# Moving the tiles of a two-layer decoder trunk to other SBUF addresses: one common start offset modulo 512 bytes

## The chip, the core and the metric

One core of a Trainium2 chip runs the whole program in one launch. The metric is the device time of that launch in microseconds (us). The profile is one profiled execution; its own time and its span (first to last instruction) are given below, beside the median of three timed runs.

## What is computed

A decoder trunk of two layers on 256 tokens of width 1024, in float32. Every sub-layer sits between two RMS norms.

```python
for l in range(2):
    h = h + 0.5 * norm(swiglu(norm(h), w_gate, w_up, w_down))    # FFN 1, width 2816
    h = h + norm(concat[pool, rglru, nsa](norm(h) @ w_in) @ w_out)  # mixer
    h = h + 0.5 * norm(swiglu(norm(h), w_gate, w_up, w_down))    # FFN 2
swiglu = (silu(x @ w_gate) * (x @ w_up)) @ w_down
```

The mixer has three branches: a causal pooling, a gated recurrence behind a short convolution, and an attention with eight heads (compressed keys, and two branches over the raw keys). The two FFNs of each layer hold nearly all of the arithmetic.

## The kernel before, in words

**Matmuls in three passes.** Each float32 operand of a large product is split into a high part (the value rounded to the format that TensorE reads at full rate, float32r) and a low part (the rest). A product is then high·high, high·low and low·high, three matmuls into one PSUM bank. `mm3` (L245) issues them as L248, L249, L250; the forms with the weights as stationary operand write the same three in a loop (L378 in `gu_cols`, L791 in `chan`). Every matmul loads its own stationary operand (128 by 128) and streams a moving operand past it.

**Which tile is which operand.** `gu_rows` (L336, tiles `pg`, `pu`) and `proj` (L544, tiles `q`, `kv`, `kw`) hold the activations `xT` stationary and stream the weights `unit`: 256 columns for `pg` and `pu`, 512 for `q` and `kv`, 280 for `kw`. `gu_cols` (L369, tiles `qg`, `qu`) and `chan` (L776, tiles `chp`, `chr`, `chg`) hold the weights `unit` stationary and stream `xT`, 256 columns in two pieces of 128 (512 bytes each). `down` (L396, tile `facc`) and `out_mm` (L899, tile `oacc`) hold `hT`, `yA`, `yL` or `yP` stationary and stream 512 columns of `unit`. Transposes (`xt`, `ht`, `pT` and others) stream the identity `ident`, which is the first 128 columns of `cn`, past 128 columns of data. The scores of the attention start with a bf16 matmul (L729) that streams `maskb` past `identb`.

**Weights.** `fetch` (L198) brings 1 MB of a weight matrix into one of three `raw` buffers on SyncE's queue; `prepare` (L212) splits it into a `unit` of a ring of five: ScalarE writes the high part (L224), VectorE the low part (L225). `pump` refills as units are released. TensorE's order is written out by hand in strings (`MIXER_ORDER`, `FFN_FIRST`, `FFN_START`, `FFN_BODY`, `FFN_END`).

**Where tiles lie.** Each tile pool takes one stretch of every partition's SBUF, in the order in which the pools are opened (L91 to L94: `cst`, `rawp`, `ringp`, `wk`), and inside a pool the tiles follow one another in the order of their first use, each size rounded up to 32 bytes. The pools begin at byte 1152 (128 modulo 512), behind a scratch area and four constants. So a tile of odd size shifts all that lie behind it. By the allocator's list of the program before, the starts modulo 512 are:

| tiles | start modulo 512 |
|---|---|
| `x0`, `x1`, `cn` (2440 bytes, the first odd size) | 128 |
| `xT` (behind `identb`, `maskb`, `caddb`, `mhalf`) | 192 |
| `gpre`, `gpost`, `kT`, first `qT` and `vv`, `bd_*` | 32 |
| second `qT` and `vv` | 128 |
| `raw`, `unit`, `yP`, `yL`, the work tiles `w0` to `w5`, the `ht` buffers (`hT`, `yA`, `pr`, `Xm`) | 224 |
| `xg`, `fg` | 352 |
| `pT` | 160 |

Slices taken from these tiles for the large matmuls are multiples of 512 bytes apart, so each operand has its tile's start modulo 512.

Of the kernel before, what the change touches and what calls it, by code (L numbers as in the profile page):

```python
# [10 lines left out]
F32 = mybir.dt.float32  # L11
F32R = mybir.dt.float32r
BF16 = mybir.dt.bfloat16
I32 = mybir.dt.int32
# [5 lines left out]
P = 128  # L20
D = 1024
KD = D // P
S = 256
NT = S // P
# [62 lines left out]
def trunk(ctx: ExitStack, tc: tile.TileContext, T, out):  # L87
    nc = tc.nc
    pe, act, dve, pool = nc.tensor, nc.scalar, nc.vector, nc.gpsimd

    cst = ctx.enter_context(tc.tile_pool(name="cst", bufs=1))  # L91
    rawp = ctx.enter_context(tc.tile_pool(name="rawp", bufs=RAW))
    ringp = ctx.enter_context(tc.tile_pool(name="ringp", bufs=RING))
    wk = ctx.enter_context(tc.tile_pool(name="wk", bufs=1))  # L94
    psp = ctx.enter_context(tc.tile_pool(name="psp", bufs=8, space=PSUM))
    ctx.enter_context(tc.manual_schedule(engines={pe.engine}))

# [10 lines left out]
        return wk.tile([P, 1024], dtype, tag="ht", name=name, bufs=5)  # L108

    def small(name, n, bufs=2):  # L110
        return wk.tile([P, n], F32, tag=name, name=name, bufs=bufs)


    x = [cst.tile([P, D], F32, name=f"x{t}") for t in range(NT)]
    cn = cst.tile([P, C_COLS], F32, name="cn")
    ident = cn[:, C_ID:C_ID + P]
    identb = cst.tile([P, P], BF16, name="identb")
    maskb = cst.tile([P, P], BF16, name="maskb")
    caddb = cst.tile([P, NT, 32], BF16, name="caddb")
    mhalf = cst.tile([P, 1], F32, name="mhalf")  # L120
    pool.memset(mhalf, -0.5)
    xT = cst.tile([P, 2, NT, KD, P], F32R, name="xT")

    def gain(kind, ap, queue=nc.sync):
        g = cst.tile([P, D], F32, tag="g" + kind, name="g" + kind)
        queue.dma_start(g, ap.partition_broadcast(P))
        return g

# [315 lines left out]

    prm = cst.tile([P, 2, 18], F32, name="prm")
    pe2 = cst.tile([P, DEPTH, 16], F32, name="pe2")
    cs = cst.tile([P, NT, 2, 32], F32, name="cs")
    lc = cst.tile([P, DEPTH, 2], F32, name="lc")
    hb = cst.tile([P, 2, 4], F32, name="hb")
    bd = {n: cst.tile([P, 2, P], F32, name="bd_" + n) for n in ("pool_w", "lru_w_r", "lru_w_i")}  # L450
    O_CW, O_CB, O_BR, O_BI, O_LAM, O_PS = 0, 8, 10, 12, 14, 16

    def load_mixer(l):
# [5 lines left out]
    def load_setup():  # L459
        rows = wk.tile([P, 256], F32, tag="yP", name="rows")  # L460
        r = 0
        for ap in (T["conv_w"].rearrange("l j c -> (l j) c"), T["conv_b"], T["lru_b_r"], T["lru_b_i"],
                   T["lru_lambda"], T["pool_scale"]):
            nc.sync.dma_start(rows[r:r + ap.shape[0], :], ap)
            r += ap.shape[0]
        per = wk.tile([32, P], F32, tag="yL", name="per")
        nc.sync.dma_start(per, T["cmp_pe"].rearrange("l (a b) d -> (l a) (b d)", b=2))
        posi = wk.tile([2, P], I32, tag="v2", name="posi")
        nc.sync.dma_start(posi, T["positions"].rearrange("o (t p) -> (o t) p", t=NT))
        return rows, per, posi  # L470

# [56 lines left out]
    def mixer(l, rs, finish):  # L528
        if l:
            load_mixer(l)  # L530
        tab, qT, gates, vsw, accs, kwps, tmp = {}, {}, {}, {}, {}, {}, {}
        kT = [cst.tile([P, 2, (t + 1) * P], F32, tag=f"kT{t}", name="kT") for t in range(NT)]
        X2 = [wk.tile([P, 2, 272], F32, tag=f"v{i}", name="X2") for i in range(2)]
        for q in X2:
            pool.memset(q[:, :, 256:272], 0.0)

# [34 lines left out]
        def q_tr(t):  # L571
            q = tmp.pop(("q", t))
            b = bank("qT")
            for i in range(4):
                pe.transpose(b[:, i * P:(i + 1) * P], q[:, i * P:(i + 1) * P], ident)
            qT[t] = cst.tile([P, 4, P], F32, tag=f"qT{t}", name="qT")
            act.activation(qT[t], b.rearrange("p (i c) -> p i c", i=4), AF.Copy)

        def kv_rope(t):
            tb, kw = tab[t], kwps[t]  # L580
            kv = accs["kv", t]
            A = w(3 * t, "kA")[:, :384].rearrange("p (h f) -> p h f", f=32)
            B = w(3 * t + 1, "kB")[:, :384].rearrange("p (h f) -> p h f", f=32)
            src = kv.rearrange("p (a x h f) -> p a x h f", a=2, x=2, f=32)[:, :, 0]
            for q, c in ((A, 2), (B, 3)):
                dve.tensor_mul(q[:, :8].rearrange("p (a h) f -> p a h f", a=2), src,
                               tb[:, c:c + 1, None, :].to_broadcast([P, 2, 4, 32]))
                dve.tensor_mul(q[:, 8:12], kw[:, :P].rearrange("p (h f) -> p h f", f=32),
                               tb[:, c:c + 1, :].to_broadcast([P, 4, 32]))
            vc = wk.tile([P, 2, 2, 64], F32, tag="pT", name="vc", bufs=4)  # L590
            act.activation(vc, kv[:, 128:256].rearrange("p (v d) -> p v d", v=2)[:, :, None, :]
                           .to_broadcast([P, 2, 2, 64]), AF.Copy, scale=rs[t][0])
            vv = cst.tile([P, 2, P], F32, tag=f"vv{t}", name="vv")
            act.activation(vv[:, 0, :], kv[:, 384:512], AF.Copy, scale=rs[t][0])
            act.activation(vv[:, 1, :], kw[:, P:2 * P], AF.Copy, scale=rs[t][0])
            vsw[t] = vv
            A = A.rearrange("p (h b) f -> p h b f", b=2)
            B = B.rearrange("p (h b) f -> p h b f", b=2)
            K = w(3 * t + 2, "kr")
            ksw = K[:, :256].rearrange("p (h b f) -> p h b f", b=2, f=32)  # L600
            dve.tensor_sub(ksw[:, :, 0, :], A[:, 2:6, 0, :], B[:, 2:6, 1, :])
            dve.tensor_add(ksw[:, :, 1, :], A[:, 2:6, 1, :], B[:, 2:6, 0, :])
            kc = K[:, 256:512].rearrange("p (v u b f) -> p v u b f", v=2, u=2, f=32)
            bc = [P, 2, 2, 32]
            dve.tensor_sub(kc[:, :, :, 0, :], A[:, 0:2, None, 0, :].to_broadcast(bc),
                           B[:, 0:2, None, 1, :].to_broadcast(bc))
            dve.tensor_add(kc[:, :, :, 1, :], A[:, 0:2, None, 1, :].to_broadcast(bc),
                           B[:, 0:2, None, 0, :].to_broadcast(bc))
            hrs = small("hr", 1)
            pool.tensor_scalar(hrs, rs[t][0], 0.5, None, op0=ALU.mult)  # L610
            g = cst.tile([P, 8, 3], F32, tag=f"gt{t}", name="gt")
            act.activation(g, kw[:, 256:280].rearrange("p (h b) -> p h b", b=3), AF.Tanh, scale=hrs)
            pool.tensor_scalar(g, g, 0.5, 0.5, op0=ALU.mult, op1=ALU.add)
            gates[t] = g
            tmp["k", t] = K, vc
# [158 lines left out]
        Y, C = {}, {}  # L774

        def chan(nm, c):  # L776
            if c == 0:
                if nm == "g":
                    C[nm] = w(5, "gl").rearrange("p (c n) -> p c n", c=2)
                else:  # L780
                    C[nm] = wk.tile([P, 2, 272], F32, tag="v2" if nm == "p" else "v3", name="x" + nm)
                    pool.memset(C[nm][:, :, :16], 0.0)
            dst = C[nm][:, c, :] if nm == "g" else C[nm][:, c, 16:]
            b = bank("ch" + nm)[:, :S]
            u = units[l, nm, 0]
            b3 = b.rearrange("p (t n) -> p t n", t=NT)
            n = 0
            for k in range(KD):
                cs_ = slice(c * P, (c + 1) * P)
                for a, h in ((0, 0), (0, 1), (1, 0)):  # L790
                    pe.matmul(b3, u[:, a, k, cs_], xT[:, h, :, k, :], start=n == 0, stop=n == 3 * KD - 1)  # L791
                    n += 1
            if c == 1:
                done((l, nm, 0))
            dve.tensor_mul(dst, b, tmp["rsB"])

        def pool_in():
            xp = C["p"]
            A = wk.tile([P, 2, 272], F32, tag="v0", name="pA")
            B = wk.tile([P, 2, 272], F32, tag="v1", name="pB")  # L800
            pool.tensor_add(A[:, :, 1:], xp[:, :, 1:], xp[:, :, :271])
            pool.tensor_add(B[:, :, 3:], A[:, :, 3:], A[:, :, 1:270])
            pool.tensor_copy(A[64:, 0, 16:], B[64:, 0, 16:])
            pool.tensor_add(A[:, 1, 7:], B[:, 1, 7:], B[:, 1, 3:268])
            pool.tensor_add(B[64:, 1, 16:], A[64:, 1, 16:], A[64:, 1, 8:264])
            pool.tensor_copy(A[64:, 1, 16:], B[64:, 1, 16:])
            pool.tensor_mul(A[:, :, 16:32], A[:, :, 16:32],
                            cn[:, C_EDGE:C_EDGE + 32].rearrange("p (c n) -> p c n", c=2))
            C["d"] = A
# [206 lines left out]
```

## Time and profile before

| | |
|---|---|
| median of 3 timed runs | 989.61 us (985.83 to 989.83) |
| the profiled execution | 989.13 us |
| its span | 987.3 us |
| TensorE matmul busy | 967.7 us, 98% |
| VectorE, ScalarE, GpSimd busy | 66%, 49%, 8% |
| HBM traffic over the span | 177 GB/s |

Busy time of TensorE counts overlapping matmuls once, and a matmul's recorded duration (0.28 us for 256 columns) is longer than the distance to the next one's start, since matmuls are pipelined. What a stream of matmuls costs is therefore read from the distance of starts, which the timeline and the chain of waits give.

### The profile page before, as it was taken

To read this page: it belongs to the slowest core of one execution; us is meant where nothing else is said; L and a number is where in the kernel's file an instruction comes from. 1 tells how busy PE (TensorE), PEld (TensorE's weight loads), DVE (VectorE), ACT (ScalarE), POOL (GpSimd) and SP (SyncE) were. 2 spreads that over 40 slices of the span, in tenths; PEclk is the share of its full clock that TensorE was granted. 3 is DMA by queue.
4 is the path that set the end of the run, shared out by engine and by line. 5 is a ranking of instruction groups with operands and counts; after the bars stand their busy time and mean duration, and the time that the engine had idled before them with its cause. 6 is when DMAs were issued, how large, how long until landed. Compare 5 with 4: busy or idle time off the path is not lost.

```text
span 987.3 us, 16105 instructions
## 1 busy us (share of the span) xinstructions
PE 967.7 (98%) x6678; PEld 881.9 (89%) x6678; DVE 646.9 (66%) x864; ACT 479.3 (49%) x760; POOL 80.5 (8%) x136
## 2 busy tenths in 40 slices
PE   6999999999999999999999999999999999999997
PEld 5999999988779999999999999998887799999996
DVE  5785555678978655655676565667698777565552
ACT  5563443457556543434454443435477465343431
POOL 2000000030034000000030000003001320000000
PEclk9999999999999999999999999999998999999999
DMA  7975565457526655555456655554762157555511
GB/s 251 337 234 203 182 202 173 151 175 171 175 68 214 203 181 181 194 180 185 157 196 233 204 179 187 194 174 140 190 187 86 43 203 246 189 195 174 192 62 43
DMA packets 131553, 176.04 MB, mean 178 GB/s; under 512 B 13156, under 2 KB 111768, under 8 KB 131480
## 3 DMA queue, kind: packets, MB, share of 16 engines
q1 hardware_dynamic: 131192, 174.43, 54.9%
q8 instruction: 52, 0.85, 0.4%
q10 hardware_dynamic: 288, 0.59, 0.2%
q14 instruction: 21, 0.17, 0.0%
HBM read 173.95 MB, written 1.05 MB: 177 GB/s over the span
## 4 chain that ended last, share of the span: by engine, by line
PE 94%; DVE 2%; ACT 2%; DMA 1%; issue 0%; DVEq 0%; POOLq 0%; ACTq 0%; SPq 0%; POOL 0%
PE qu L378 21%; PE qg L378 21%; PE facc L250 8%; PE facc L249 8%; PE facc L248 8%; PE pu L248 2%; PE pu L250 2%; PE pu L249 2%; PE oacc L248 2%; PE oacc L249 1%; PE oacc L250 1%; PE pg L249 1%; PE pg L250 1%; PE pg L248 1%; PE yT L763 1%; PE chp L791 1%
## 5 line engine op out<-in xcount | busy, mean ns | idle before, releaser
L224 ACT ACTIVATE unit<-raw 128x1024 fp32r<-128x1024 f32 (+2 forms) x320 | 322.7, 1033 | 353.6 <-issue 296.6
L225 DVE TENSOR_TENSOR unit<-raw,unit 128x1024 fp32r<-128x1024 f32 (+2 forms) x320 | 375.9, 1195 | 139.8 <-ACT unit L224 139.5
L378 PEld LDWEIGHTS qg<-xT,unit 128*128 128x128 f32 x1728 | 208.9, 188 | 2.2
L378 PE MATMUL qu<-xT,unit 128*128 128x256 f32 x1728 | 210.7, 281 | 0.0
L378 PE MATMUL qg<-xT,unit 128*128 128x256 f32 x1728 | 210.3, 281 | 0.0
L378 PEld LDWEIGHTS qu<-xT,unit 128*128 128x128 f32 x1728 | 207.0, 188 | 0.0
L248 PE MATMUL facc<-unit,hT 128*128 128x512 f32 x352 | 137.7, 391 | 0.0
L250 PE MATMUL facc<-unit,hT 128*128 128x512 f32 x352 | 137.6, 391 | 0.0
L249 PE MATMUL facc<-unit,hT 128*128 128x512 f32 x352 | 137.5, 391 | 0.0
L250 PEld LDWEIGHTS facc<-unit,hT 128*128 128x128 f32 x352 | 66.1, 188 | 14.0
L248 PEld LDWEIGHTS facc<-unit,hT 128*128 128x128 f32 x352 | 66.2, 188 | 12.9
L249 PEld LDWEIGHTS facc<-unit,hT 128*128 128x128 f32 x352 | 66.1, 188 | 13.1
L388 DVE TENSOR_TENSOR gp<-qg,rsB 128x512 f32<-128x512 f32 x36 | 24.8, 690 | 65.0 <-PE qg L378 65.0
L264 POOL TENSOR_TENSOR mspost<-ev,s 128x1 f32<-128x1 f32 x8 | 4.7, 591 | 670.8 <-ACT sq L258 670.8
L393 DVE SCALAR_TENSOR_TENSOR h<-qu,m 128x512 f32<-128x512 f32 x36 | 24.9, 691 | 52.1 <-PE qu L378 52.1
L249 PE MATMUL pg<-unit,xT 128*128 128x256 f32 x128 | 36.9, 288 | 1.6 <-DVE unit L225 1.5
L248 PE MATMUL pg<-unit,xT 128*128 128x256 f32 x128 | 36.8, 287 | 0.4 <-ACT unit L224 0.4
L250 PE MATMUL pg<-unit,xT 128*128 128x256 f32 x128 | 36.3, 284 | 0.0
L248 PE MATMUL pu<-unit,xT 128*128 128x256 f32 x128 | 36.2, 282 | 0.0
L249 PE MATMUL pu<-unit,xT 128*128 128x256 f32 x128 | 35.8, 280 | 0.0
L250 PE MATMUL pu<-unit,xT 128*128 128x256 f32 x128 | 35.6, 278 | 0.0
L739 ACT ACTIVATE pr<-s,mx 128x128 f32<-128x128 f32 (+1 forms) x64 | 26.1, 433 | 3.7 <-DVE mx L737 3.6
(259 smaller groups left out, 1164.3 us busy)
## 6 DMA issues: line engine op xcount, KB each, us to landing
raw<-in_ffn_w_down_dram SPq DMA_DIRECT2D x44, 1024.0 KB, 5.4
raw<-in_ffn_w_gate_dram SPq DMA_DIRECT2D x42, 1024.0 KB, 5.2
raw<-in_ffn_w_up_dram SPq DMA_DIRECT2D x42, 1024.0 KB, 5.2
raw<-in_w_in_dram SPq DMA_DIRECT2D x14, 1024.0 KB, 5.1
raw<-in_w_out_dram SPq DMA_DIRECT2D x4, 1024.0 KB, 5.0
raw<-in_w_out_dram SPq DMA_DIRECT2D x8, 512.0 KB, 6.4
raw<-in_w_in_dram SPq DMA_DIRECT2D x4, 560.0 KB, 3.7
raw<-in_ffn_w_up_dram SPq DMA_DIRECT2D x4, 512.0 KB
```

The source lines that it names most:

```text
L224: act.activation(u[:, 0, i:i + step], r[:, i:i + step], AF.Copy)
L225: dve.tensor_sub(u[:, 1, i:i + step], r[:, i:i + step], u[:, 0, i:i + step].bitcast(F32))
L248: pe.matmul(o, sh, mh, start=first and i == 0, stop=False)
L249: pe.matmul(o, sh, ml, start=False, stop=False)
L250: pe.matmul(o, sl, mh, start=False, stop=last and i == n - 1)
L264: pool.tensor_add(m, eps, s2[:, 0:1])
L378: pe.matmul(o3, u[:, a, k, bs], xT[:, h, :, k, :], start=n == 0, stop=n == 3 * KD - 1)
L388: dve.tensor_tensor(b2(gp), b2(g), tmp["rsB"][:, None, :].to_broadcast([P, 2, S]), op=ALU.mult)
L393: dve.scalar_tensor_tensor(h, u, 0.5, m, op0=ALU.mult, op1=ALU.mult)
L739: act.activation(prs[v][:, b0 + i, :], sb[v][:, i, :], AF.Exp, bias=mx[:, i:i + 1], accum_out=cf[:, v, b0 + i:b0 + i + 1])
L763: pe.matmul(YT[t][v * 64:(v + 1) * 64, :], vsw[kb][:, br, v * 64:(v + 1) * 64], PT.pop((t, br, v, kb)), start=False, stop=br == 1 and kb == t,
L791: pe.matmul(b3, u[:, a, k, cs_], xT[:, h, :, k, :], start=n == 0, stop=n == 3 * KD - 1)
```

## The change

No instruction is added, removed or reordered; pools and the tiles' membership in them change. A new pool `lead` (416 bytes: `identb` 256, `caddb` 128, `mhalf` 4 rounded to 32) comes first, so that what follows begins at 1152 + 416 = 1568, which is 32 modulo 512. A new pool `big` comes behind it and holds tiles of `cst` whose sizes are multiples of 512; `rawp`, `ringp` and `wk` follow, `wk` without its odd-sized tiles; `cst`, with all odd sizes, is opened last. By these sizes every tile of `big`, `rawp`, `ringp` and `wk` starts at 32 modulo 512, and so does `cn`, the first tile of `cst`. `maskb`, `kk` and the tiles of the tags `v0` to `v3` lie behind `cn` at other offsets.

```diff
-    cst = ctx.enter_context(tc.tile_pool(name="cst", bufs=1))
+
+    lead = ctx.enter_context(tc.tile_pool(name="lead", bufs=1))
+    big = ctx.enter_context(tc.tile_pool(name="big", bufs=1))
     rawp = ctx.enter_context(tc.tile_pool(name="rawp", bufs=RAW))
     ringp = ctx.enter_context(tc.tile_pool(name="ringp", bufs=RING))
     wk = ctx.enter_context(tc.tile_pool(name="wk", bufs=1))
+    cst = ctx.enter_context(tc.tile_pool(name="cst", bufs=1))
...
     def small(name, n, bufs=2):
-        return wk.tile([P, n], F32, tag=name, name=name, bufs=bufs)
-
-
-    x = [cst.tile([P, D], F32, name=f"x{t}") for t in range(NT)]
+        return (wk if n % 128 == 0 else cst).tile([P, n], F32, tag=name, name=name, bufs=bufs)
+
+
+    identb = lead.tile([P, P], BF16, name="identb")
+    caddb = lead.tile([P, NT, 32], BF16, name="caddb")
+    mhalf = lead.tile([P, 1], F32, name="mhalf")
+    xT = big.tile([P, 2, NT, KD, P], F32R, name="xT")
+    x = [big.tile([P, D], F32, name=f"x{t}") for t in range(NT)]
     cn = cst.tile([P, C_COLS], F32, name="cn")
     ident = cn[:, C_ID:C_ID + P]
-    identb = cst.tile([P, P], BF16, name="identb")
     maskb = cst.tile([P, P], BF16, name="maskb")
-    caddb = cst.tile([P, NT, 32], BF16, name="caddb")
-    mhalf = cst.tile([P, 1], F32, name="mhalf")
     pool.memset(mhalf, -0.5)
-    xT = cst.tile([P, 2, NT, KD, P], F32R, name="xT")
...
-        g = cst.tile([P, D], F32, tag="g" + kind, name="g" + kind)
+        g = big.tile([P, D], F32, tag="g" + kind, name="g" + kind)
...
-    cs = cst.tile([P, NT, 2, 32], F32, name="cs")
+    cs = big.tile([P, NT, 2, 32], F32, name="cs")
...
-    bd = {n: cst.tile([P, 2, P], F32, name="bd_" + n) for n in ("pool_w", "lru_w_r", "lru_w_i")}
+    bd = {n: big.tile([P, 2, P], F32, name="bd_" + n) for n in ("pool_w", "lru_w_r", "lru_w_i")}
...
-        posi = wk.tile([2, P], I32, tag="v2", name="posi")
+        posi = cst.tile([2, P], I32, tag="v2", name="posi")
...
-        kT = [cst.tile([P, 2, (t + 1) * P], F32, tag=f"kT{t}", name="kT") for t in range(NT)]
-        X2 = [wk.tile([P, 2, 272], F32, tag=f"v{i}", name="X2") for i in range(2)]
+        kT = [big.tile([P, 2, (t + 1) * P], F32, tag=f"kT{t}", name="kT") for t in range(NT)]
+        X2 = [cst.tile([P, 2, 272], F32, tag=f"v{i}", name="X2") for i in range(2)]
...
```

In the same way `qT` and `vv` go from `cst` to `big`, and the tiles `xp`, `xr`, `pA` and `pB` of the tags `v0` to `v3` from `wk` to `cst`. Tags and buffer counts stay as they are, and all tiles that share a buffer move together.

## Rows read from the trace of the kernel before

**Rows 1.** The page: span, busy time, TensorE's granted clock, HBM, the chain that ended last.

```profile
span 987.3 us, 16105 instructions
...
PE 967.7 (98%) x6678; PEld 881.9 (89%) x6678; DVE 646.9 (66%) x864; ACT 479.3 (49%) x760; POOL 80.5 (8%) x136
...
PEclk9999999999999999999999999999998999999999
...
HBM read 173.95 MB, written 1.05 MB: 177 GB/s over the span
...
PE 94%; DVE 2%; ACT 2%; DMA 1%; issue 0%; DVEq 0%; POOLq 0%; ACTq 0%; SPq 0%; POOL 0%
```

**Rows 2.** Groups of TensorE by form: line, tiles, sizes, count | busy us, mean ns.

```profile
L378 PE MATMUL qu<-xT,unit 128*128 128x256 f32 x1728 | 210.7, 281 | 0.0
L378 PE MATMUL qg<-xT,unit 128*128 128x256 f32 x1728 | 210.3, 281 | 0.0
L248 PE MATMUL facc<-unit,hT 128*128 128x512 f32 x352 | 137.7, 391 | 0.0
...
L248 PE MATMUL pg<-unit,xT 128*128 128x256 f32 x128 | 36.8, 287 | 0.4 <-ACT unit L224 0.4
...
L248 PE MATMUL oacc<-unit,yA 128*128 128x512 f32 x32 | 13.0, 405 | 0.0
...
L248 PE MATMUL q<-unit,xT 128*128 128x512 f32 x32 | 12.6, 395 | 0.0
...
L791 PE MATMUL chp<-xT,unit 128*128 128x256 f32 x96 | 12.4, 285 | 0.0
...
L248 PE MATMUL kw<-unit,xT 128*128 128x280 f32 x32 | 9.3, 291 | 0.0
```

**Rows 3.** The chain in order of time: start us, us, what. Transposes and weights-stationary matmuls.

```profile
36.81 5.68 PE qg L378 x48
42.49 0.44 PE ht L365 x4
...
958.83 5.68 PE qu L378 x48
```

**Rows 4.** Timeline of TensorE: two matmuls of 512 bf16 columns: start us, us of both.

```profile
232.80 0.59 PE L729 MATMUL s<-maskb,identb 128*128 128x512 bf16 x2
```

**Rows 5.** Timeline of TensorE: 512 columns, xT stationary, first and last of 16 in a row.

```profile
208.30 0.40 PE L249 MATMUL kv<-unit,xT 128*128 128x512 f32 x1
...
211.80 0.40 PE L249 MATMUL kv<-unit,xT 128*128 128x512 f32 x1
```

**Rows 6.** Timeline of TensorE: 512 columns, first and last of 15 (hT) and 10 (yL).

```profile
346.77 0.39 PE L249 MATMUL facc<-unit,hT 128*128 128x512 f32 x1
...
349.94 0.39 PE L248 MATMUL facc<-unit,hT 128*128 128x512 f32 x1
...
299.94 0.39 PE L250 MATMUL oacc<-unit,yL 128*128 128x512 f32 x1
...
301.99 0.39 PE L250 MATMUL oacc<-unit,yL 128*128 128x512 f32 x1
```

**Rows 7.** Timeline of TensorE: xT stationary, first and last of 18 (pu) and 22 (kw).

```profile
329.88 0.28 PE L248 MATMUL pu<-unit,xT 128*128 128x256 f32 x1
...
331.88 0.29 PE L250 MATMUL pu<-unit,xT 128*128 128x256 f32 x1
...
219.27 0.29 PE L248 MATMUL kw<-unit,xT 128*128 128x280 f32 x1
...
221.97 0.29 PE L248 MATMUL kw<-unit,xT 128*128 128x280 f32 x1
```

**Rows 8.** TensorE's work on unit by stretch: us, busy (x), granted clock, DMA share, GB/s.

```profile
36.90:42.40 5.50, 5.50 (x48) 1.00 1.00 352
958.90:964.40 5.50, 5.50 (x49) 1.00 0.01 3
```

**Rows 9.** Waits of TensorE and of SyncE's queue: who for whom: us, times, longest.

```profile
PE xt L308 <- DMA cn<-in_consts_dram: 7.0, 1, 7.0
PE yT L717 <- ACT pcT L712: 2.3, 2, 1.1
...
SPq L207 <- DVE unit L225: 704.9, 138, 16.9
```

More of the change, by code (lines that the diff above doesn't have):

```diff
@@ L575, in q_tr @@
                 pe.transpose(b[:, i * P:(i + 1) * P], q[:, i * P:(i + 1) * P], ident)
-            qT[t] = cst.tile([P, 4, P], F32, tag=f"qT{t}", name="qT")
+            qT[t] = big.tile([P, 4, P], F32, tag=f"qT{t}", name="qT")
             act.activation(qT[t], b.rearrange("p (i c) -> p i c", i=4), AF.Copy)
@@ L592, in kv_rope @@
                            .to_broadcast([P, 2, 2, 64]), AF.Copy, scale=rs[t][0])
-            vv = cst.tile([P, 2, P], F32, tag=f"vv{t}", name="vv")
+            vv = big.tile([P, 2, P], F32, tag=f"vv{t}", name="vv")
             act.activation(vv[:, 0, :], kv[:, 384:512], AF.Copy, scale=rs[t][0])
@@ L780, in chan @@
                 else:
-                    C[nm] = wk.tile([P, 2, 272], F32, tag="v2" if nm == "p" else "v3", name="x" + nm)
+                    C[nm] = cst.tile([P, 2, 272], F32, tag="v2" if nm == "p" else "v3", name="x" + nm)
                     pool.memset(C[nm][:, :, :16], 0.0)
@@ L798, in pool_in @@
             xp = C["p"]
-            A = wk.tile([P, 2, 272], F32, tag="v0", name="pA")
-            B = wk.tile([P, 2, 272], F32, tag="v1", name="pB")
+            A = cst.tile([P, 2, 272], F32, tag="v0", name="pA")
+            B = cst.tile([P, 2, 272], F32, tag="v1", name="pB")
             pool.tensor_add(A[:, :, 1:], xp[:, :, 1:], xp[:, :, :271])
```

## The prediction

> **What bounds the kernel now.** I read the page first. TensorE is busy for 98% of the span and makes 94% of the chain that ended last; VectorE is at 66%, ScalarE at 49%, and the granted clock is at its upper level, 2.4 GHz, in all but one of the forty slices [rows 1]. The waits of TensorE are short: 7.0 us once at the start for a DMA, then 2.3 us and less per group [rows 9]. So the end is set by how closely matmuls follow one another, and no other engine's work is worth anything here unless it grows by a third.
>
> The second view is the list of forms, for the counts [rows 2]. Each line shown stands for its passes and its twins: 3456 matmuls of `gu_cols` and 288 of `chan` (3744 with 256 columns, weights stationary), 768 of `gu_rows` (256 columns, `xT` stationary), 192 of `q` and `kv` (512 columns, `xT` stationary), 96 of `kw` (280 columns), and 1056 of `facc` with 192 of `oacc` (1248 with 512 columns; `hT`, `yA`, `yL` or `yP` stationary). The mean durations in that view are longer than the distance of starts and are not used.
>
> The third view is the distance of starts.
> - Weights stationary, 256 columns: 48 matmuls take 5.68 us, 118.3 ns each, early and late in the program alike [rows 3]. One such stretch has the DMA engines fully busy and the other has them at 0.01, and the pace is the same [rows 3, 8]; traffic of DMA is not what sets it.
> - `xT` stationary: 512 columns, 3.50 us over 15 steps, 233.3 ns [rows 5]; 256 columns, 2.00 us over 17, 117.6 ns; 280 columns, 2.70 us over 21, 128.6 ns [rows 7].
> - `hT` stationary, 512 columns: 3.17 us over 14 steps, 226.4 ns. `yL` stationary: 2.05 us over 9, 227.8 ns [rows 6].
>
> At 2.4 GHz one column a cycle would be 213.3, 116.7 and 106.7 ns for 512, 280 and 256 columns. Two bf16 matmuls of 512 columns do come 0.21 us apart (0.59 less one duration of 0.38) [rows 4], and transposes, which load 128 columns of weights for 128 moving ones, come 0.11 us apart (0.44 over 4) [rows 3], so neither the array nor the weight load alone asks for more. What is above is an excess that only float32r streams show: 11.6 ns (`gu_cols`, `chan`), 10.9 (`gu_rows`), 11.9 (`kw`), 20.0 (`q`, `kv`) and 13.1 (`facc`, `oacc`). Summed over the counts this is 3744 × 11.6 + 768 × 10.9 + 96 × 11.9 + 192 × 20.0 + 1248 × 13.1 = 73 us, the pot out of which the change can take anything.
>
> **Why a place can count.** `kv` and `facc` stream the same kind of tile from the same offset (224) with the same 512 columns. They differ in the stationary tile: `xT` at 192 in the one, `hT` at 224 in the other. The first costs 6.9 ns more for every matmul [rows 5, 6], and `yL`, also at 224, goes with `hT` [rows 6]. So the pace does depend on where the stationary tile lies. Two readings fit: the distance between the starts of the two operands (32 bytes apart is bad, level is better), or the place of `xT` itself. The change answers both, since it puts `xT`, `unit`, `hT` and the `y` tiles level, at 32.
>
> The rule that speaks against this is in the Trainium skill, "TensorE: Matmul & The Clock Gate", under "Step-by-step: what each phase is for": "Loading the next tile's weights doesn't steal SBUF read bandwidth from the running matmul." By that rule the stationary tile's place would count for nothing and the sum would be zero; the 6.9 ns between two forms that differ in it disagree.
>
> **The change part by part.** Nothing is added or removed, so every term is a change of pace times a count.
>
> 1. `q` and `kv`: operands come level as those of `facc` are. From 233.3 to 226.4 ns, 192 × 6.9 = 1.3 us saved.
> 2. `facc` and `oacc`: level before, level after. I take 0. Bounds: if the place itself is worth something, down to 213.3 (1248 × 13.1 = 16.3 us saved) or up to the 233.3 of `kv` (8.6 us lost).
> 3. `gu_cols` and `chan`, the large term. Before, the moving tile is at 192 and the stationary at 224. No row has 256 columns with level operands. Nearest rows: going level took the excess at 512 columns from 20.0 to 13.1, a factor of 0.66. Applied to 11.6 this leaves 7.7, so 114.4 ns, and 3744 × 3.9 = 14.6 us saved. A second way agrees: at one placement, `kv` against `pu`, half the columns have 0.55 of the excess (10.9 against 20.0), so the level 13.1 becomes 7.2, or 113.9 ns. I take 114.4. Bounds: 110 ns, the pace of transposes, below which weight loads would not go (31 us saved), and 126.7, the whole excess of `kv` on every weight load (31 us lost).
> 4. `gu_rows` and `kw`: 10.9 and 11.9 by the same factor give 113.9 and 124.6 ns; 768 × 3.7 + 96 × 4.0 = 2.8 + 0.4 = 3.2 us saved. Bounds in proportion.
> 5. Transposes, scores and the other small forms: `ident` goes from 128 to 32. Weight loads set their pace, 0.11 us for whatever offset the data has, so nothing.
> 6. DMA: `raw` goes from 224 to 32, the same number of bytes by the same issues. SyncE's queue waits 704.9 us for buffers that VectorE has to release [rows 9], so a slower landing is hidden by the loads that are issued ahead; without that cover the price would be the longer landing at each of some 160 loads. I take 0.
> 7. VectorE, ScalarE, GpSimd: same instructions. Tiles that share a buffer move together with their tags and counts, so no wait is added on any queue. If TensorE runs 2% faster, VectorE at 66% and a stream that wants 177 GB/s where 352 is reached [rows 1, 8] still keep up.
>
> Sum: 1.3 + 0 + 14.6 + 3.2 = 19.1 us off the chain, nearly all inside stretches in which TensorE never waits. The profiled execution took 989.1 us, half a microsecond under the median of the runs, 989.6. So 970.0 against its own time, and 970.5 against the median. **I predict 970 us.**
>
> **The rivals.**
>
> *The excess goes altogether.* If 32 is a clean place for each stream by itself and not only level with its partner, 256 columns fall to the transposes' 110 ns and 512 to 213.3: 3744 × 8.3 + 768 × 7.6 + 192 × 20.0 + 1248 × 13.1 + 96 × 10.6 = 31.1 + 5.8 + 3.8 + 16.3 + 1.0 = 58 us, so 931 (`kw` down to 118.0, in proportion to its columns). For it: bf16 streams show almost no excess [rows 4]. Against it: `facc` is level already and keeps 13.1 ns [rows 6]. Part of it, 940 to 955, is likelier than all.
>
> *Nothing happens.* The 6.9 ns could belong to something that the layout leaves alone, such as the shape of `xT`'s slices or the time at which its weight load begins, and 256-column streams could have a fixed cost. The time stays at 989.6. For it: excesses of 10.9 to 11.9 for three forms with 256 to 280 columns in two different placements look alike [rows 3, 7]. This is where the skill's rule would lead.
>
> *Level operands collide more at 256 columns.* The next weight load and the moving stream start together. With 512 columns the load is over when half the stream has gone by, with 256 the stream has no second half in which to recover. If the level excess belongs to each weight load and not to the columns, it is the whole 13.1 for every matmul, and the pace becomes 119.8 ns: 3744 × 1.5 + 768 × 2.2 + 96 × 1.2 − 1.3 = 6.1 us more, so 995.7; with the 20.0 of `kv` it would be as much as 1037. It decides as soon as 256 columns come out over 118.3 ns. Against it: at one placement the excess of 256 columns is about half that of 512, so it goes by columns so far [rows 5, 7].
>
> **How the numbers follow.** Forecast 0.43 (its own range 958 to 982), the larger gain 0.22, nothing 0.16, collisions 0.19. A measurement of this kernel can tell about 0.5%, 4.9 us, from no change. Faster: the first two and a little of the edge, 0.66; same 0.16; slower 0.18. The range goes from 940 (leaving out about 0.1 for the excess gone nearly altogether) to 998 (leaving out about 0.1 for the dearer collisions).
>
> **What would show it.** In the chain of waits of the changed kernel the pieces of 48 `qg` matmuls should take 5.49 us and not 5.68 (5.28 by the larger gain, 5.68 by no effect, 5.75 by collisions). In the timeline `kv` should step by 226 ns, `facc` still by 226, `pu` by 114. TensorE's waits and the clock should be as before. I am wrong if `qg` keeps its pace, if `facc` moves by more than 2 ns, or if the gain is eaten by new waits of TensorE for `unit`.

## The result: 0.6% slower, and the profile after

The changed kernel takes 993.69 us (median of five runs, 991.98 to 996.35) against 986.52 for the kernel before in the same session (median of five, 985.83 to 989.83): a ratio of 1.0057 on record (the quotient of the two medians is 1.0073), 95% interval 1.0033 to 1.0081. The forecast was 970 us and faster; 993.69 lies inside the range of 940 to 998, but the sign is wrong.

The page of the changed kernel shows the same program with TensorE busy for 8.1 us longer, VectorE's time unchanged, and the same shape of the chain, to be read against [rows 1]. It is the page of the slowest of the five runs (996.35 us), with a mean granted clock of 0.993 against 0.996 before, so part of the 8.1 us is clock; the change is therefore read from steps inside stretches at the upper level.

```profile
span 994.3 us, 16105 instructions
...
PE 975.8 (98%) x6678; PEld 890.7 (90%) x6678; DVE 647.1 (65%) x864; ACT 478.6 (48%) x760; POOL 80.6 (8%) x136
...
PE 94%; DVE 2%; ACT 2%; DMA 1%; issue 0%; DVEq 0%; POOLq 0%; ACTq 0%; SPq 0%; POOL 0%
```

The waits of the changed kernel (who for whom: us, times, longest) are those of [rows 9]; the time did not come from a new wait.

```profile
PE xt L311 <- DMA cn<-in_consts_dram: 7.0, 1, 7.0
PE yT L720 <- ACT pcT L715: 2.4, 2, 1.2
...
SPq L210 <- DVE unit L228: 712.6, 140, 16.9
```

The chain of the changed kernel in order of time (start us, us, what) answers to [rows 3], and says where the time came from: 48 matmuls with 256 columns take 5.76 us instead of 5.68.

```profile
37.03 5.76 PE qg L381 x48
43.45 5.76 PE qu L381 x48
...
965.84 5.76 PE qu L381 x48
```

The timeline of TensorE in the changed kernel, first and last of a row of 15 `kv`, 33 `pu` and 18 `facc` matmuls, answers to [rows 5 to 7].

```profile
211.48 0.39 PE L251 MATMUL kv<-unit,xT 128*128 128x512 f32 x1
...
214.66 0.39 PE L253 MATMUL kv<-unit,xT 128*128 128x512 f32 x1
...
331.12 0.28 PE L251 MATMUL pu<-unit,xT 128*128 128x256 f32 x1
...
334.96 0.28 PE L253 MATMUL pu<-unit,xT 128*128 128x256 f32 x1
...
349.97 0.39 PE L252 MATMUL facc<-unit,hT 128*128 128x512 f32 x1
...
353.83 0.39 PE L251 MATMUL facc<-unit,hT 128*128 128x512 f32 x1
```

The steps are 3.18/14 = 227 ns (`kv`, 233.3 before), 3.84/32 = 120.0 ns (`pu`, 117.6 before) and 3.86/17 = 227 ns (`facc`, as before). All 256-column matmuls of the two weight-times-activation forms now go at the same 120.0 ns.

In the distance of starts the result is accounted for: 3744 × (120.0 − 118.3) + 768 × (120.0 − 117.6) − 192 × (233.3 − 226.7) = 6.4 + 1.8 − 1.3 = 6.9 us. The medians differ by 7.2, and the interval of the ratio allows 3.3 to 8.0 us; the agreement is closer than the times alone could show. The 96 `kw` matmuls (280 columns) take no part: 24 of them, from 220.33 to 223.29 us in the same timeline, step by 2.96/23 = 128.7 ns, against 128.6 before. Their slices of `unit` are 280 × 4 = 1120 bytes apart, so only the first has its tile's start modulo 512 (ahead of the prediction I said it of all large matmuls), and the change could not bring the others level.

### The profile page after: what moved, and what is told of

It is laid out like the page before. It is cut to its first block, busy times and chain, and to the rows that moved or that the text cites. A ratio compares the mean times of both kernels' runs of the same rounds, so it can differ in the third digit from the quotient of the medians.

```text
span 994.3 us, 16105 instructions
## 1 busy us (share of the span) xinstructions
PE 975.8 (98%) x6678; PEld 890.7 (90%) x6678; DVE 647.1 (65%) x864; ACT 478.6 (48%) x760; POOL 80.6 (8%) x136
## 4 chain that ended last, share of the span: by engine, by line
PE 94%; DVE 2%; ACT 2%; DMA 1%; issue 0%; DVEq 0%; POOLq 0%; ACTq 0%; SPq 0%; POOL 0%
PE qu L381 21%; PE qg L381 21%; PE facc L251 8%; PE facc L252 8%; PE facc L253 8%; PE pg L252 2%; PE pu L251 2%; PE pu L253 2%; PE pu L252 2%; PE oacc L251 2%; PE pg L253 1%; PE oacc L253 1%; PE oacc L252 1%; PE pg L251 1%; PE yT L766 1%; PE chp L794 1%
## 5 line engine op out<-in xcount | busy, mean ns | idle before, releaser
L381 PEld LDWEIGHTS qg<-xT,unit 128*128 128x128 f32 x1728 | 211.6, 192 | 2.2
L381 PE MATMUL qu<-xT,unit 128*128 128x256 f32 x1728 | 213.5, 283 | 0.0
L381 PE MATMUL qg<-xT,unit 128*128 128x256 f32 x1728 | 213.0, 283 | 0.0
L381 PEld LDWEIGHTS qu<-xT,unit 128*128 128x128 f32 x1728 | 209.9, 192 | 0.0
L252 PE MATMUL pg<-unit,xT 128*128 128x256 f32 x128 | 37.6, 294 | 0.6 <-DVE unit L228 0.5
L251 PE MATMUL pg<-unit,xT 128*128 128x256 f32 x128 | 37.4, 292 | 0.4 <-ACT unit L227 0.4
L253 PE MATMUL pg<-unit,xT 128*128 128x256 f32 x128 | 37.1, 290 | 0.0
```

Of the source, the lines that this page charges most:

```text
L251: pe.matmul(o, sh, mh, start=first and i == 0, stop=False)
L252: pe.matmul(o, sh, ml, start=False, stop=False)
L253: pe.matmul(o, sl, mh, start=False, stop=last and i == n - 1)
L381: pe.matmul(o3, u[:, a, k, bs], xT[:, h, :, k, :], start=n == 0, stop=n == 3 * KD - 1)
```

## Experiments

Kernels of this section are the changed kernel with one edit, unless it says otherwise. "Level" means that the stationary and the moving operand of a matmul start at the same offset modulo 512. A distance is the moving tile's start less the stationary one's; moving `xT` by d bytes puts `qg` and `qu` (which stream `xT`) at +d and `pu`, `pg`, `q`, `kv` (which stream `unit` past `xT`) at −d. Before, `qg` was at −32 and `pu` at +32. The kernel before, run on the same chips beside these kernels, took between 988.6 and 990.5 us (its single runs between 985.8 and 992.0), so a single time of a kernel tells little by itself, and the pace in its trace is what is read. A kernel is called timed where it was run several times and has a ratio.

### Is it the place or the distance?

```diff
-    mhalf = lead.tile([P, 1], F32, name="mhalf")
+    mhalf = cst.tile([P, 1], F32, name="mhalf")
```

> The changed kernel with mhalf moved out of the leading pool, so that all large operands are level at 0 modulo 512 instead of 32. Distance theory (only the distance between the starts of the stationary and the moving operand counts): the pieces of 48 qg matmuls stay at 5.76 us (120.0 ns each), facc and kv at 226.7 ns, time 990 to 996 us. Place theory (32 is itself a bad offset): the pieces change by at least 0.1 us, to 5.3 to 5.65 us, and the time with them.

Measured: 995.28 us. The chain has the level pace again:

```profile
37.68 5.76 PE qg L381 x48
...
964.81 5.76 PE qu L381 x48
```

So 32 is neither a better nor a worse place than 0.

```diff
+    padx = ctx.enter_context(tc.tile_pool(name="padx", bufs=1))
+    xtp = ctx.enter_context(tc.tile_pool(name="xtp", bufs=1))
+    pady = ctx.enter_context(tc.tile_pool(name="pady", bufs=1))
...
+    padh = ctx.enter_context(tc.tile_pool(name="padh", bufs=1))
+    hp = ctx.enter_context(tc.tile_pool(name="hp", bufs=1))
...
-    xT = big.tile([P, 2, NT, KD, P], F32R, name="xT")
+    xT = xtp.tile([P, 2, NT, KD, P], F32R, name="xT")
-        return wk.tile([P, 1024], dtype, tag="ht", name=name, bufs=5)
+        return hp.tile([P, 1024], dtype, tag="ht", name=name, bufs=5)
...
+    pool.memset(padx.tile([P, 64], F32, name="padx"), 0.0)
+    pool.memset(pady.tile([P, 64], F32, name="pady"), 0.0)
+    pool.memset(padh.tile([P, 64], F32, name="padh"), 0.0)
```

The pads, 256 bytes each, lie ahead of `xT`, behind it and ahead of the `ht` buffers.

> The changed kernel with xT and the ht buffers (hT, yA, pr, Xm) 256 bytes further on, at 288 modulo 512, all else at 32. Distance theory: half a period apart is as far as two operands can be, so the pace should leave the level values; by the rule that 32 bytes apart (before) gave less excess at 256 columns than level, 5.3 to 5.68 us for 48 qg matmuls and 213 to 233 ns for kv and facc, time 940 to 990 us. Place theory: only the moved tiles' own offset counts, so pu and qg change but in kind like before; no number. Fixed cost of 13.3 ns per weight load wherever tiles lie: 5.76 us and 226.7 ns, time 993 us.

Measured: 996.84 us, and the chain:

```profile
37.32 5.76 PE qg L389 x48
...
966.11 5.76 PE qu L389 x48
```

The distance theory as I had put it (half of 512 is as far as it goes) missed: 256 apart goes at the pace of level. The place theory has nothing for the same pace in two kernels, one with all large tiles at another place and one with `xT` and the `ht` buffers elsewhere. The fixed cost wherever tiles lie foretold this pace, but not the 118.3 ns of the kernel before; the next kernel decides on it. What is left of the distance theory is one with a period of 256 bytes or less.

### Which tile, and is there anything else in the layout?

```diff
-    xT = big.tile([P, 2, NT, KD, P], F32R, name="xT")
+    xT = xtp.tile([P, 2, NT, KD, P], F32R, name="xT")
...
+    pool.memset(padx.tile([P, 120], F32, name="padx"), 0.0)
+    pool.memset(pady.tile([P, 8], F32, name="pady"), 0.0)
```

The pools are the first three of the kernel before this; the pads are now 480 bytes ahead of `xT` and 32 behind it.

> The changed kernel with xT alone put 32 bytes short of level again (at 0, unit at 32), its distance before; hT and the rest stay level. If level operands of the 256-column matmuls are the cause, 48 qg matmuls take 5.66 to 5.70 us again instead of 5.76, kv goes back from 226.7 to 231 to 234 ns, and the time to 985 to 989 us, ratio to before 0.997 to 1.003. If something else in the new layout costs the time (DMA landing, the small tiles' places, the order of pools), the time stays at 992 to 996.

Measured, timed: 987.44 us against 988.59, ratio 0.9994 (0.9978 to 1.0009). The chain and the timeline (first and last of 15 `kv`, of 32 `pu`):

```profile
36.31 5.68 PE qg L386 x48
...
955.26 5.68 PE qu L386 x48
```

```profile
209.69 0.39 PE L256 MATMUL kv<-unit,xT 128*128 128x512 f32 x1
...
212.96 0.39 PE L258 MATMUL kv<-unit,xT 128*128 128x512 f32 x1
...
327.54 0.28 PE L256 MATMUL pu<-unit,xT 128*128 128x256 f32 x1
...
331.15 0.28 PE L257 MATMUL pu<-unit,xT 128*128 128x256 f32 x1
```

With `xT` alone put back to its old distance, `qg` is at 118.3 ns and `kv` at 3.27/14 = 233.6, as before, and the loss is gone. A fixed cost wherever tiles lie is thereby refuted. `pu` is at 3.61/31 = 116.5, not at the 117.6 of before [rows 7], although the distance is the same +32 (the starts are now at 0 and 32 modulo 512 and were at 192 and 224). The place need not be the reason, for the kernel before has both paces itself, with its tiles where they are. Its first 96 `pu`, from first to last:

```profile
25.45 0.28 PE L248 MATMUL pu<-unit,xT 128*128 128x256 f32 x1
...
36.53 0.28 PE L250 MATMUL pu<-unit,xT 128*128 128x256 f32 x1
```

That is 11.08/95 = 116.6 ns. So one layout can settle on more than one pace; nothing here tells what picks one. The other moves of the change (DMA targets, small tiles, the order of pools) cost nothing that can be measured.

```diff
-        return wk.tile([P, 1024], dtype, tag="ht", name=name, bufs=5)
+        return hp.tile([P, 1024], dtype, tag="ht", name=name, bufs=5)
...
+    pool.memset(padh.tile([P, 120], F32, name="padh"), 0.0)
```

480 bytes now lie ahead of the `ht` buffers (pools `padh` and `hp` as in the kernel 256 apart), and `xT` is where the change put it.

> The changed kernel with the ht buffers alone put 32 bytes short of level (at 0, unit at 32). Distance theory: the 1056 facc matmuls take the off-level pace of kv before, 231 to 234 ns instead of 226.7, and the time rises by 5 to 8 us to 998 to 1003; qg stays at 5.76 us. If 512 columns are not made slower by distance (kv before was slow because of xT's own place), facc stays at 226.7 and the time at 993 to 996.

Measured: 998.86 us. First and last of 14 `facc` matmuls in the timeline:

```profile
75.35 0.40 PE L254 MATMUL facc<-unit,hT 128*128 128x512 f32 x1
...
78.39 0.39 PE L255 MATMUL facc<-unit,hT 128*128 128x512 f32 x1
```

3.04/13 = 234 ns, the pace of `kv` before. So 512 columns are better level, and 256 columns are better 32 bytes off: the two widths want opposite things. That is the whole reason for the wrong sign.

### Is the level excess a constant of 13 ns?

Level, 256 columns take 120.0 ns and 512 take 226.7, each 13.3 ns over one column a cycle at 2.4 GHz. That looks like the constant of the third rival. Two kernels with fewer columns tested it.

```diff
-                        pe.matmul(o3, u[:, a, k, bs], xT[:, h, :, k, :], start=n == 0, stop=n == 3 * KD - 1)
+                        m = 124 if n else P
+                        pe.matmul(o3[:, :, :m], u[:, a, k, bs], xT[:, h, :, k, :m], start=n == 0, stop=n == 3 * KD - 1)
...
+                if c:
+                    js = slice(j * 512, j * 512 + 504)
+                o = acc[t][j][:, :504] if c else acc[t][j]
-                mm3(acc[t][j], [(q[0][k], q[1][k], u[:, 0, k, js], u[:, 1, k, js]) for k in range(2)],
+                mm3(o, [(q[0][k], q[1][k], u[:, 0, k, js], u[:, 1, k, js]) for k in range(2)],
```

> The changed kernel with 504 of the 512 columns streamed in all facc matmuls but those of the first two chunks' first group (chunk 0), and 124 of each 128 tokens in all but the first qg and qu matmul of each group: the left out columns lack part of their sum. All starts stay level. A fixed 13.3 ns (16 cycles at 1.2 GHz) on top of the columns of each matmul: facc 223.3 ns (252 + 16 cycles), qg 116.7 ns, 48 in 5.60 us. Starts held to a grid of 13.3 ns when level (259 cycles rounded up to 272, 131 to 144): facc 213.3 ns (255 rounded up to 256), qg stays at 120.0 ns (weight load of 131 cycles rounded up to 144), 5.76 us.

Measured: 983.30 us. First and last of 14 `facc` in the timeline, and the chain:

```profile
63.75 0.39 PE L251 MATMUL facc<-unit,hT 128*128 128x504 f32 x1
...
66.70 0.39 PE L252 MATMUL facc<-unit,hT 128*128 128x504 f32 x1
```

```profile
67.31 5.48 PE qg L382 x48
72.79 5.49 PE qu L382 x48
```

Both theories missed both forms. 504 columns keep 2.95/13 = 227 ns, the pace of 512; 248 columns take 114.4 ns, less than either said. A constant excess is refuted, and so is the grid of 13.3 ns.

```diff
-            for j, js in enumerate(HALF):
-                mm3(acc[t][j], [(q[0][k], q[1][k], u[:, 0, k, js], u[:, 1, k, js]) for k in range(2)],
+            for j in range(2):
+                m = 512 - 8 * (c + 1) if c else 512
+                js = slice(j * 512, j * 512 + m)
+                mm3(acc[t][j][:, :m], [(q[0][k], q[1][k], u[:, 0, k, js], u[:, 1, k, js]) for k in range(2)],
```

> The changed kernel with the columns streamed by facc cut chunk by chunk: 512 in chunk 0, then 496, 488, 480, 472, 464, 456, 448, 440, 432, 424 in chunks 1 to 10; the columns left out lack those terms. All starts stay level. Grid theory (level starts fall on a grid of 16 cycles of 1.2 GHz, 13.3 ns, and a matmul needs its columns at two a cycle plus 4 to 16 cycles): plateaus at 226.7, 213.3 and 200.0 ns, so neighbouring widths share a pace and 480 columns take 213.3, 448 take 200.0. Line theory (a fixed excess): 3.3 ns less with each 8 columns fewer, 220.0 at 496, 213.3 at 480, 200.0 at 448, 190 at 424. Conflict by length (504 columns kept 226.7 since their length breaks the pattern): no plateaus and no line, and the widths that are multiples of 64 columns (448) do better or worse than their neighbours by over 5 ns.

Measured: 976.49 us. The timeline, first and last of 14 at 496, 488 and 448 columns:

```profile
57.90 0.38 PE L251 MATMUL facc<-unit,hT 128*128 128x496 f32 x1
...
60.76 0.38 PE L252 MATMUL facc<-unit,hT 128*128 128x496 f32 x1
...
74.70 0.38 PE L251 MATMUL facc<-unit,hT 128*128 128x488 f32 x1
...
77.56 0.38 PE L252 MATMUL facc<-unit,hT 128*128 128x488 f32 x1
...
157.75 0.36 PE L251 MATMUL facc<-unit,hT 128*128 128x448 f32 x1
...
160.39 0.36 PE L252 MATMUL facc<-unit,hT 128*128 128x448 f32 x1
```

Steps: 220.0 ns at 496 and at 488, 203 at 448. In between, from the same view: 216.6 (480), 213.4 (472), 208.9 (464), 208.8 (456). There are pairs that share a pace, but no stairs of 13.3 ns and no line.

The same widths with the `ht` buffers moved as in the kernel with `hT` off level:

> The same widths with the ht buffers 32 bytes short of level. Grid theory: the grid belongs to level operands, so the pace falls by about 3.3 ns for each 8 columns from 233.3 at 512, with no plateaus: about 226 at 496, 207 at 448, 197 at 424. If the excess off level goes by columns (20 of 213.3 ns), 3.6 ns for each step.

Measured: 977.22 us.

```profile
57.98 0.39 PE L254 MATMUL facc<-unit,hT 128*128 128x496 f32 x1
...
60.90 0.39 PE L255 MATMUL facc<-unit,hT 128*128 128x496 f32 x1
...
157.96 0.37 PE L254 MATMUL facc<-unit,hT 128*128 128x448 f32 x1
...
160.65 0.37 PE L255 MATMUL facc<-unit,hT 128*128 128x448 f32 x1
```

225 ns at 496 and 207 at 448; from the same view 220.0 (488), 219.9 (480), 213.3 (472), 211.2 (464), 208.8 (456). The ends are near those of the falling line forecast for this kernel (226 at 496, 207 at 448), but 488 and 480 share a pace, which the line excludes. Off level is slower at 512, 496, 480, 464 and 448 columns, the multiples of 16, and equal within 0.2 ns at 488, 472 and 456, which are not. Distance and length act together, and none of my three theories gives both series.

### Does the next weight load's reading take part?

```diff
-                        pe.matmul(o3, u[:, a, k, bs], xT[:, h, :, k, :], start=n == 0, stop=n == 3 * KD - 1)
+                        m = 64 if 0 < n < 3 * KD - 1 else P
+                        pe.matmul(o3[:m], u[:, a, k, b * P:b * P + m], xT[:, h, :, k, :], start=n == 0, stop=n == 3 * KD - 1)
...
-                mm3(acc[t][j], [(q[0][k], q[1][k], u[:, 0, k, js], u[:, 1, k, js]) for k in range(2)],
+                m = 64 if 0 < c < NC - 1 else P
+                mm3(acc[t][j][:m], [(q[0][k][:, :m], q[1][k][:, :m], u[:, 0, k, js], u[:, 1, k, js]) for k in range(2)],
```

> The changed kernel with 64 instead of 128 columns of the stationary operand in the facc matmuls of chunks 1 to 9 and in all but the first and last qg and qu matmul of each group: the other rows of the output lack those terms. All starts stay level. If the excess comes of the next weight load reading beside the stream, half the load brings about half of it: facc 218 to 221 ns, qg 111 to 115 ns. If it belongs to the moving stream or to the start of a matmul, facc stays at 226.7 and qg at 120.0 ns.

Measured: 979.10 us. The chain, and first and last of 14 `facc`:

```profile
39.17 5.48 PE qg L382 x48
45.30 5.49 PE qu L382 x48
```

```profile
59.12 0.39 PE L251 MATMUL facc<-unit,hT 128*64 128x512 f32 x1
...
62.11 0.40 PE L252 MATMUL facc<-unit,hT 128*64 128x512 f32 x1
```

Half the load brings `qg` from 120.0 to 114.2 ns, as the conflict theory said, but `facc` gets slower, 2.99/13 = 230 ns. That the excess is proportional to the bytes of the load is refuted. The edit also halves the rows of output that each matmul writes, which was not tried apart, so it is not shown that the load is what moves both paces.

### The map of distances

Two kernels gave each slice of `xT` its own distance (the second also put a pool of 32 bytes behind `xT`).

```diff
-    xT = big.tile([P, 2, NT, KD, P], F32R, name="xT")
+    xT = big.tile([P, 2, NT, KD, 144], F32R, name="xT")[:, :, :, :, :P]
...
-            sq = wk.tile([P, 512], BF16, tag="sq", name="sq", bufs=2)
+            sq = wk.tile([P, 512], BF16, tag="sq", name="sq", bufs=1)
```

> xT with 576 bytes from one slice of 128 columns to the next instead of 512, so that slice k lies 64k bytes (modulo 512) from level; the two tiles of tokens and the two halves stay level with each other. One of the two buffers of sq is given up for the room. Distance theory: the steps of pu and qg differ by slice, with 120.0 ns at slice 0 and some distances below 115 ns. Fixed cost per weight load: 120.0 ns for every slice. A rule by 64-byte steps alone (32 off is what matters): 120.0 ns for every slice too.

> As the even sweep, with everything behind xT 32 bytes further on, so that slice k lies 64k minus 32 bytes from level. Distance theory: slice 0 of qg goes as in the kernel before (about 118.3 ns), the others differ by slice. Fixed cost per weight load: 120.0 ns for every slice. A rule by 64-byte steps alone: 117 to 118.5 ns for every slice.

Measured: 988.72 and 987.61 us; 48 `qg` matmuls take 5.65 to 5.68 us in the first and 5.69 to 5.71 in the second. Slice by slice the median step was 117 to 119 ns (even) and 117 to 120 ns (odd), and slice 0 of the even sweep, which is level, went at 119 ns, not at 120.0. A mixture hides what a single distance does. These two were inconclusive, beyond ruling out the constant, and wrong as a guide: in the odd sweep the slices at +96 went at 117 to 118 ns, where a whole kernel takes 120.0, and a slice at +32 went at 120, where a whole kernel takes 116.7.

So each distance got a kernel of its own, with the tile of `xT` made 512 bytes longer and its view begun d bytes further on (here 32):

```diff
-    xT = big.tile([P, 2, NT, KD, P], F32R, name="xT")
+    xTw = big.tile([P, 2 * NT * KD * P + 128], F32R, name="xT")
+    xT = xTw[:, 8:8 + 2 * NT * KD * P].rearrange("p (h t k c) -> p h t k c", h=2, t=NT, k=KD)
```

> The changed kernel with xT alone 16 bytes beyond level. If any distance that is no multiple of 256 bytes frees the 256-column matmuls from the level pace, qg goes at 117 to 119 ns (48 in 5.62 to 5.71 us), kv at 230 to 235, time 985 to 990 us. If only distances of 32 bytes and more count, all stays as level: 5.76 us, 226.7 ns, 993 us. A pace of 114 ns or less would make it a version faster than both.

Measured: 986.76 us; `qg` and `qu` 5.69 to 5.71 us for 48 in 69 of 72 pieces (118.8 ns), 5.45 in two. A distance of 16 bytes is enough to leave the level pace.

> The changed kernel with xT alone 64 bytes beyond level. From the sweeps, where slice by slice mixed distances gave 117.8 ns at 64: 48 qg in 5.62 to 5.71 us, kv 229 to 235 ns, time 984 to 990 us. If a 64-byte multiple is as bad as level: 5.76 us and 993 us.

> The changed kernel with xT alone 64 bytes beyond level, timed. If the pace is a matter of the distance between the operands alone, qg keeps the 5.66 us for 48 of the single look, against 5.68 before and 5.76 changed, and rows of pu 117.5 ns or less; the time 983 to 987 us, ratio to before 0.994 to 0.999. If the single look at 983.9 us was luck of the granted clock, the ratio is 0.998 to 1.002.

Measured: 983.88 us in the first run; timed, 984.84 us against 990.47, ratio 0.9943 (0.9929 to 0.9957), and `qg` at 117.8 ns:

```profile
37.26 5.66 PE qg L382 x48
...
954.60 5.65 PE qu L382 x48
```

This one kernel was profiled twice, and the two traces differ in a stretch. The first 96 `pu` of the first run:

```profile
25.29 0.28 PE L252 MATMUL pu<-unit,xT 128*128 128x256 f32 x1
...
36.06 0.28 PE L254 MATMUL pu<-unit,xT 128*128 128x256 f32 x1
```

That is 10.77/95 = 113.4 ns; the same 96 step by 11.19/95 = 117.8 in the other trace, the pace of all later `pu` in both. The pace expected for them, 117.5 or less, is missed by the usual one.

> The changed kernel with xT alone 32 bytes beyond level: the mirror of before, where it lies 32 short. Before, the moving operand of pu lay 32 beyond the stationary one and that of qg 32 short of it. If the sign counts (the 140-cycle pattern of pu, 116.7 ns, belongs to a moving operand 32 beyond), qg now takes 116.7 ns (48 in 5.60 us) and pu 118.3, time 980 to 985 us, ratio 0.992 to 0.997. If the sign does not count, qg stays at 118.3 (5.68 us) and the time at 985 to 989.

Measured, timed: 981.90 us against 990.47, ratio 0.9917 (0.9900 to 0.9933). The chain, and the timeline with first and last of 32 `pu`:

```profile
61.28 5.60 PE qg L382 x48
...
954.19 5.60 PE qu L382 x48
```

```profile
328.93 0.28 PE L252 MATMUL pu<-unit,xT 128*128 128x256 f32 x1
...
332.59 0.28 PE L253 MATMUL pu<-unit,xT 128*128 128x256 f32 x1
```

`qg` takes 5.60/48 = 116.7 ns, `pu` 3.66/31 = 118 ns: the two have changed places against the kernel with `xT` 32 short. The sign counts, and the large form now has the good side. This version beats both kernels; by the two ratios, each to the kernel before, it is 1.4% faster than the changed one (1.0057/0.9917), which differs from it in where the view of `xT` begins and in that tile's length.

> The changed kernel with xT alone 128 bytes beyond level, as far from level as it goes if the period is 256 bytes. If the pace improves with distance from level: qg below 117 ns (48 under 5.62 us). If every distance off level is alike: 5.64 to 5.71 us, kv 230 to 235 ns, 984 to 990 us.

Measured: 995.34 us, which neither half of the expectation had; `qg` and `qu` at the level pace in 64 of 72 pieces:

```profile
37.12 5.70 PE qg L382 x48
...
964.84 5.76 PE qu L382 x48
```

> The changed kernel with xT alone 192 bytes beyond level, that is 64 short of the next level if the period is 256. Same as 64 beyond with the roles of pu and qg exchanged: 48 qg in 5.64 to 5.71 us, pu near 117.5 ns, 983 to 989 us. If the period were 512, it would differ from both sides of level, with no number.

Measured: 980.93 us in one run, near the kernel 32 beyond and faster than expected. Of 72 pieces 66 take 5.65 or 5.66 us, six 5.46:

```profile
36.60 5.66 PE qg L382 x48
42.91 5.46 PE qu L382 x48
```

Part of that gain is `kv` at 229 ns, and the `chan` matmuls, 48 `chr` in 5.46 us. That 42.91 us piece (113.8 ns) is a settled pace beside the usual one again.

> The changed kernel with xT alone 96 bytes beyond level, one of the two steps of 32 bytes still unseen as a whole kernel. In the odd sweep slices at 96 took 116 to 118 ns and, every third time, 125, among other distances. If a whole kernel at 96 is like the middle of those: 48 qg in 5.65 to 5.75 us, time 984 to 992 us. If a common distance lets the pattern settle on the 116 ns: 5.57 to 5.60 us and 979 to 983 us, a rival to 32 beyond.

> The changed kernel with xT alone 160 bytes beyond level, the other one unseen. If the pattern at 128 (near level: 120 and 118.8 ns) repeated the one at 0, 160 would repeat the one at 32: 48 qg in 5.60 us, pu near 118.3 ns, time 980 to 985 us. If the period is 256, it is a distance of its own, by the odd sweep (118.9 ns) 5.66 to 5.76 us and 985 to 993 us.

Measured: 993.45 and 990.69 us, `qg` at 5.76 and 5.70 us for 48. So 96 is as slow as level, by neither of its expectations, 160 does not repeat 32 and the period is not 128.

The map for 256 columns gives the usual pace in ns per matmul, `qg` and `qu` from the pieces of 48 (most of them), `pu` from 47 steps in a row of the timeline:

```
distance modulo 256     0      16     32     64     96     128    160    192    224
qg, qu                120.0  118.8  116.7  117.8  120.0  120.0  118.8  117.8  118.3
pu                    120.0    -    116.8  117.7  120.0  118.5  118.5  117.7  118.3
```

Except at 128, where both paces occur, `qg` and `pu` agree within 0.3 ns at the same distance, though the one streams `xT` in two pieces past `unit` and the other `unit` in one piece past `xT`. The distance, moving less stationary, modulo 256, is what the usual pace of 256 columns follows. In the kernel before, which is not in the map, `qg` fits it (118.3 at −32); `pu`, at +32, fits it with its first 96 (116.6) and not with the later ones (117.6).

## Why the prediction was wrong

- **What bounds the kernel** held: the waits are as before, and the whole difference lies in the distance of starts.
- **"Why a place can count"** held in kind: the stationary tile's place counts. Of its two readings the first (distance) carries the large form and the second (`xT`'s own place) fell with the kernels level at 0 and 256 apart; the 1.1 ns of `pu` between the old layout and the kernel with `xT` 32 short are no sign of it, since stretches of the kernel before differ by as much. By the sentence of the Trainium skill ("TensorE: Matmul & The Clock Gate", "Step-by-step: what each phase is for") that loading the next weights takes no read bandwidth from the running matmul, the stationary tile's place would not count; `facc` at 227 ns with `hT` level and at 234 with `hT` 32 short disagrees.
- **Part 1** (`q`, `kv`: 226.4 ns forecast) was right: 227 measured, 1.3 us saved. **Part 2** (`facc` unchanged) was right.
- **Part 3 is the step that failed**, and part 4 with it: "Applied to 11.6 this leaves 7.7, so 114.4 ns". I took the one pair of rows that showed what level does, at 512 columns, and scaled it to 256 as if the excess had a sign and a proportion that hold for every width. Level took 512 columns from 233.3 to 226.7, but 256 columns from 118.3 to 120.0: −14.6 us forecast, +6.4 us by the measured steps. In part 4 `gu_rows` went to 120.0 ns and not to 113.9, and `kw` stayed where it was; most of its slices are not level in either kernel. My second way ("half the columns have 0.55 of the excess") agreed only because it compared `kv` and `pu` at one spacing of the tiles, where they sit at the same distance; it said nothing on level.
- **Parts 5 to 7** (transposes, DMA, other engines at nothing) held: with `xT` alone moved back, the ratio to before is 0.9994.
- **The rival "level operands collide more at 256 columns"** was the one that came true, in direction and in size: 119.8 ns and 6.1 us more, against 120.0 and 7.2. That 993.69 lies inside the range is owed to this rival, which I gave 0.19, and not to the sum. Its point of decision, 256 columns over 118.3 ns, is the line that the chain crosses. Its picture of a constant per weight load was not confirmed: 504 columns cost as much as 512, and the kernel with half a load has `facc` slower. So its number was met in part by luck.
- **The rival "the excess goes altogether"** is refuted: it wanted 110 ns, the usual pace was 116.7 or more at every distance, and the fastest stretches seen were at 113 to 114. (Its 118.0 ns for `kw` is not in proportion to the columns, which would be 120.3; that is 0.2 us of its 58.)

What stays open is why. The runs show that the pace follows the distance between the stationary operand, which the weight load reads, and the moving one, with a period of 256 bytes, and that it depends on length. How the two act on each other is not shown: a model that gives 120.0, 116.7, 226.7 and 233.3 together was not found, nor what picks one of two settled paces.

## What to carry to other kernels

Where TensorE is the bound with float32r operands, measure the distance of starts for each width and each distance of the two operands before giving every tile one alignment: here level was best for 512 columns and among the worst for 256, and 32 bytes between the tiles moved the kernel by 1.4%. A factor read off one matmul width is no forecast for another. Give each distance a kernel of its own, since mixed distances in one stream show neither the best nor the worst pace.

## What the runs showed that was not expected

- The sign of the distance counts: 116.7 ns at +32, 118.3 at −32 (3744 matmuls: 6 us).
- 256 bytes apart equals level (5.76 us for 48), 128 apart nearly does, 160 does not repeat 32.
- One layout can settle on two paces: 96 `pu` at 113.4 ns in one run of a kernel and at 117.8 in another.
- Fewer columns can cost nothing: `facc` at 504 columns keeps the 226.7 ns of 512, and 488 shares the 220.0 ns of 496.
- With half the weight columns (and half the output rows) 512 columns get slower: `facc` from 226.7 to 230 ns.
